# A two-layer transformer trunk: four mixed weight pairs per chunk instead of three, one weight sum made by an adding DMA, and a new layout of the weights

## The chip, the cores and the metric

The kernel runs on one core of one Trainium2 chip. The metric is the time of one execution on the device in microseconds (us). The engines are named as in the profile: PE multiplies matrices, DVE and ACT work element by element, POOL is GpSimd, and SP issues most of the DMAs.

## The reference

Two layers, each with a mixer (two kinds of attention between an input and an output projection) and a SwiGLU block, all in float32 on 256 tokens of width 2048. The change touches the SwiGLU block and the way in which weights are loaded:

```python
D_MODEL = 2048; SEQ = 256; DEPTH = 2
D_FF = (-(-8 * D_MODEL // 3) + 255) // 256 * 256          # 5632

def swiglu(h, w_gate, w_up, w_down):
    return (jax.nn.silu(h @ w_gate) * (h @ w_up)) @ w_down

for l in range(DEPTH):
    h = rms_norm(x, pre_mix_norm[l])
    m = hybrid_mixer(h, l, w_in[l], w_o[l], ...)
    x = x + rms_norm(m, post_mix_norm[l])
    h = rms_norm(x, pre_ffn_norm[l])
    f = swiglu(h, w_gate[l], w_up[l], w_down[l])
    x = x + rms_norm(f, post_ffn_norm[l])
```

## The kernel before

**Splitting.** A float32 operand goes to PE in two parts: ACT rounds it to the multiplier's format (`hi`, L176), DVE subtracts (`lo = raw - hi`, L178), and a product of an activation (sh, sl) with a weight (hi, lo) is three matmuls: sh·hi, sh·lo, sl·hi (`product`, L706 to L708; `unit` in the projections, L352 to L354).

**Weights.** All weights stand in one list, `stream`, in the order of use. An entry is a pair of K tiles: 256 rows by 512 columns, 512 KB, which SP loads into a tile `raw` of 128 partitions by 2 x 512 (L139). There are four `raw` tiles; a load waits until one is free again, that is, until `lo` or the last sum that reads it is done. There are six `hi` and six `lo` tiles. `feed` splits up to four entries ahead of the one that is used (`LOOKAHEAD`). The tile framework plans the order in which each engine issues its instructions; each engine then runs its own list strictly in that order and waits by semaphores.

**Gate and up.** The 5632 columns are done in 11 chunks of 512. In a chunk, for each of 8 K pairs `kp`, a gate entry and an up entry are used. The plain way (`eight`) is eight products (2 K tiles x 2 token tiles x gate and up), 24 matmuls. The other way (`seven`) takes the 2 x 2 blocks of tokens and K tiles against K tiles and gate/up as a 2 x 2 matrix product by Strassen's scheme in Winograd's form: seven products, 21 matmuls. For that it needs four sums of activations, made once per pair and layer (`pair_sums`, `token_sums`), and four sums of weights per chunk and pair (`mixed_weights`). With g0, g1 the two K tiles of gate and u0, u1 those of up they are t1 = g0 + u0, t3 = u0 + u1, t2 = t1 + u1, t4 = t2 + g1. DVE adds them (L150) into tiles `T`, and ACT and DVE split them into `Th` (L159) and `Tl` (L161); u1 is split alone (L154, L155). In chunk 0 the pairs 4 and 6 go by seven products (`FIRST_SEVEN`), in the chunks 1 to 10 the pairs 2, 4 and 6 (`SEVEN`). Four of the seven products are shared by several outputs; they add up in banks of their own (p1, p6, p7, q5) over the pairs of a chunk, and `shared_part` and the end of the chunk add them to the four results (L743 to L747, L853 to L856). Four banks serve the results of a chunk and the other four its shared products, and the roles change with each chunk.

**Down.** Two halves of 1024 columns; in each, 6 of the 22 pairs (`DOWN_SEVEN`) go by seven products, with the weights mixed by the same function.

**Order around the change.** SP issues the loads in stream order. ACT issues `hi`, then for a mixed entry `Th`; DVE issues the sums, `lo` and `Tl`. POOL makes masks at the opening and applies the rotation of the differential heads (`rotate`, L570 to L573), and issues no DMA.

The program's function and its callers:

Of the kernel before, what the change touches and what calls it, by code (L numbers as in the profile page):

```python
# [9 lines left out]
F32 = mybir.dt.float32  # L10
# [7 lines left out]
P = 128  # L18
D = 2048
S = 256  # L20
L = 2
# [14 lines left out]
SEVEN = (2, 4, 6)  # L36
FIRST_SEVEN = (4, 6)
FIRST_ORDER = (0, 1, 3, 2, 4, 5, 6, 7)
FORM_AT = {1: 4, 3: 6, 5: 2}
# [9 lines left out]

@with_exitstack  # L50
def kernel(
# [3 lines left out]
    w_in: bass.AP,  # L55
    w_o: bass.AP,
# [6 lines left out]
    w_gate: bass.AP,  # L63
    w_up: bass.AP,
    w_down: bass.AP,
    rope: bass.AP,
    x_columns: bass.AP,
    gain_columns: bass.AP,
    out: bass.AP,
# [21 lines left out]
    stream = []  # L91

    def queue_pair(w2d, kp, c):
        stream.append(
            w2d[kp * 2 * P : (kp + 1) * 2 * P, c * CW : (c + 1) * CW].rearrange("(k p) n -> p k n", p=P)
        )
        return len(stream) - 1

    plan = []
    sevens = set()  # L100
    for l in range(L):
        lay = {"in": {}, "o": {}, "gate": {}, "up": {}, "down": {}}
        chunks = []
        for g in range(2):
            chunks += [6 + g, 8 + g, 10 + g]
        for g in range(2):
            chunks += [g, 2 + g, 4 + g]
        lay["chunks"] = chunks
        for c in chunks:
            for kp in range(KT // 2):  # L110
                lay["in"][c, kp] = queue_pair(w_in[l], kp, c)
        order_o = [(c, kp) for kp in KP_O for c in (0, 1)]
        order_o += [(c, kp) for c in (2, 3) for kp in range(KT // 2)]
        lay["order_o"] = order_o
        for c, kp in order_o:
            lay["o"][c, kp] = queue_pair(w_o[l], kp, c)
        for c in range(FF // CW):
            for kp in FIRST_ORDER if c == 0 else range(KT // 2):
                lay["gate"][c, kp] = queue_pair(w_gate[l], kp, c)
                lay["up"][c, kp] = queue_pair(w_up[l], kp, c)  # L120
                if kp in (FIRST_SEVEN if c == 0 else SEVEN):
                    sevens.add(lay["up"][c, kp])
        for half in range(2):
            for kp in range(FF // P // 2):
                for c in (2 * half, 2 * half + 1):
                    lay["down"][c, kp] = queue_pair(w_down[l], kp, c)
                if kp in DOWN_SEVEN:
                    sevens.add(lay["down"][2 * half + 1, kp])
        plan.append(lay)
# [5 lines left out]
    def fetch(upto):  # L135
        while len(raws) < min(upto, len(stream)):
            i = len(raws)
            raw = wpool.tile([P, 2, CW], F32, tag="raw", bufs=4, name=f"raw{i}")
            loads.append(nc.sync.dma_start(raw, stream[i]))  # L139
            raws.append(raw)  # L140
# [3 lines left out]
    def mixed_weights(i):  # L144

        g, u = raws[i - 1], raws[i]
        sums = [mix_pool[0].tile([P, 2, CW], F32, tag="T", bufs=2, name=f"T{i}_{j}") for j in range(2)]
        t1, t3, t2, t4 = sums[0][:, 0, :], sums[0][:, 1, :], sums[1][:, 0, :], sums[1][:, 1, :]
        for o, a, b in ((t1, g[:, 0, :], u[:, 0, :]), (t3, u[:, 0, :], u[:, 1, :]), (t2, t1, u[:, 1, :]), (t4, t2, g[:, 1, :])):
            nc.vector.tensor_tensor(out=o, in0=a, in1=b, op=ALU.add)  # L150
        parts = []
        hi = wpool.tile([P, 2, CW], F32R, tag="hi", bufs=6, name=f"hi{i}")
        lo = wpool.tile([P, 2, CW], F32R, tag="lo", bufs=6, name=f"lo{i}")
        nc.scalar.activation(hi[:, 1, :], u[:, 1, :], AF.Copy)  # L154
        nc.vector.tensor_tensor(out=lo[:, 1, :], in0=u[:, 1, :], in1=hi[:, 1, :].bitcast(F32), op=ALU.subtract)  # L155
        parts.append((hi[:, 1, :], lo[:, 1, :]))
        for j in range(2):
            th = mix_pool[0].tile([P, 2, CW], F32R, tag="Th", bufs=3, name=f"Th{i}_{j}")
            nc.scalar.activation(th, sums[j], AF.Copy)  # L159
            tl = mix_pool[0].tile([P, 2, CW], F32R, tag="Tl", bufs=3, name=f"Tl{i}_{j}")  # L160
            nc.vector.tensor_tensor(out=tl, in0=sums[j], in1=th.bitcast(F32), op=ALU.subtract)  # L161
# [53 lines left out]
    setup = tc.alloc_tile_pool(name="setup", bufs=1, side="right", reuse_waits="tile")  # L215
    idle = setup.tile([P, CW], BF16, name="idle")
# [10 lines left out]
    lams = setup.tile([P, 4, L * 64], F32, name="lams")  # L227
    negones = setup.tile([P, P], F32, name="negones")
# [6 lines left out]
    def late_constants():  # L235
# [16 lines left out]
        lprod = setup.tile([P, 2, L * 64], F32, name="lprod")  # L252
        lsum = setup.tile([P, 2, L], F32, name="lsum")
# [761 lines left out]
```

## Time and profile before

| | us |
|---|---|
| median of three runs (lowest, highest) | 2225.18 (2224.80, 2225.68) |
| the profiled execution, its time on the device | 2225.4 |
| its span, first to last instruction | 2223.6 |
| first gate and up stage, from its first matmul to the first of down | 402.3 to 877.1 |
| second gate and up stage, first to last matmul | 1509.8 to 1982.4 |

The mean granted PE clock over the span is 0.998. A row of the profile names line, engine, operation, output and inputs, and shape; "mean ns of one" runs from an instruction's start to its end, and instructions of an engine can overlap, so their distance can be shorter than that. "Idle before" is the time that the engine stood before these instructions, with what ended it. A row of windows gives the busy time of each engine between two times.

### The profile page before, as it was taken

Reading aid. Unit: us, or ns where it says so; the run is one execution under the profiler, and the core shown is the slowest. Engines: PE = TensorE matmul, PEld = TensorE weight load, DVE = VectorE, ACT = ScalarE, POOL = GpSimd, SP = SyncE. Lnnn points to the kernel's source line nnn. Section 1 sums busy time; section 2 is a strip of 40 time slices with the busy share of each in tenths; the row PEclk is TensorE's granted clock in tenths of the full one; section 3 lists DMA queues with packets and bytes.
Section 4 is the critical chain, followed back from the end, with each engine's and each line's share of the span. In section 5 each row is a group of like instructions: output and inputs, shape, how many; then the busy total and the mean of one; then the engine's idle time right before and its main releaser. Section 6 shows DMA issues by size and latency. Waiting matters only on the chain.

```text
span 2223.6 us, 28156 instructions
## 1 busy us (share of the span) xinstructions
PE 2205.6 (99%) x10117; PEld 1814.4 (82%) x10117; DVE 1765.9 (79%) x2505; ACT 1276.3 (57%) x1895; POOL 37.4 (2%) x76
## 2 busy tenths in 40 slices
PE   9999999999999999999999999999999999999998
PEld 7888888788888888888877888887888888888886
DVE  6666555899889989989876665558998898999897
ACT  6555554656555556656565455546655555566563
POOL 1100000000000000000010000000000000000000
PEclk9999999999999999999999999999999999999999
DMA  8655555466665665656555555554666565566564
GB/s 292 194 164 165 159 189 183 138 208 203 204 199 190 205 207 189 213 189 213 194 182 170 169 163 161 183 187 151 201 207 202 178 221 194 190 212 211 183 217 143
DMA packets 217996, 423.72 MB, mean 191 GB/s; under 512 B 13568, under 2 KB 14080, under 8 KB 217344
## 3 DMA queue, kind: packets, MB, share of 16 engines
q1 hardware_dynamic: 217712, 421.91, 58.8%
q8 instruction: 79, 1.29, 0.2%
q14 instruction: 61, 0.50, 0.1%
q10 hardware_dynamic: 144, 0.02, 0.0%
HBM read 419.77 MB, written 2.10 MB: 190 GB/s over the span
## 4 chain that ended last, share of the span: by engine, by line
PE 94%; ACT 2%; DVE 1%; DMA 1%; issue 0%; SPq 0%; DVEq 0%; ACTq 0%
PE c L707 10%; PE c L706 10%; PE c L708 10%; PE in L352 8%; PE in L354 8%; PE in L353 8%; PE dn L911 5%; PE dn L909 5%; PE dn L908 5%; PE o L354 2%; PE o L352 2%; PE o L353 2%; PE p L706 2%; PE p L707 2%; PE p L708 2%; ACT hi L176 1%
## 5 line engine op out<-in xcount | busy, mean ns | idle before, releaser
L178 DVE TENSOR_TENSOR lo<-raw,hi 128x1024 fp32r<-128x1024 f32 x695 | 843.9, 1224 | 309.6 <-ACT hi L176 304.4
L176 ACT ACTIVATE hi<-raw 128x1024 fp32r<-128x1024 f32 x695 | 726.9, 1056 | 497.8 <-PE in L354 164.9
L706 PE MATMUL c<-hi,xF 128*128 128x512 f32 x960 | 377.0, 394 | 1.4 <-ACT w L743 0.8
L707 PE MATMUL c<-lo,xF 128*128 128x512 f32 x960 | 373.9, 390 | 1.1 <-DVE lo L178 1.0
L708 PE MATMUL c<-hi,xF 128*128 128x512 f32 x960 | 374.0, 391 | 0.0
L159 ACT ACTIVATE Th<-T 128x1024 fp32r<-128x1024 f32 x176 | 185.7, 1056 | 141.7 <-DVE T L150 133.8
L161 DVE TENSOR_TENSOR Tl<-T,Th 128x1024 fp32r<-128x1024 f32 x176 | 214.2, 1217 | 4.4 <-ACT Th L159 3.8
L706 PEld LDWEIGHTS c<-hi,xF 128*128 128x128 f32 x960 | 180.5, 188 | 39.2 <-ACT w L743 1.2
L707 PEld LDWEIGHTS c<-lo,xF 128*128 128x128 f32 x960 | 180.6, 188 | 38.5 <-DVE lo L178 2.3
L708 PEld LDWEIGHTS c<-hi,xF 128*128 128x128 f32 x960 | 180.7, 188 | 37.8
L908 PE MATMUL dn<-hi,jh 128*128 128x512 f32 x464 | 180.7, 389 | 0.0
L909 PE MATMUL dn<-lo,jh 128*128 128x512 f32 x464 | 180.5, 389 | 0.0
L352 PE MATMUL in<-hi,xI 128*128 128x512 f32 x384 | 154.0, 401 | 0.4 <-ACT xI L293 0.4
L352 PE MATMUL in<-hi,xT 128*128 128x512 f32 x384 | 153.8, 401 | 0.5 <-ACT hi L176 0.5
L354 PE MATMUL in<-hi,xI 128*128 128x512 f32 x384 | 150.3, 391 | 0.3 <-DVE xI L298 0.3
L353 PE MATMUL in<-lo,xI 128*128 128x512 f32 x384 | 150.0, 391 | 0.5 <-DVE lo L178 0.5
L353 PE MATMUL in<-lo,xT 128*128 128x512 f32 x384 | 149.8, 390 | 0.5 <-DVE lo L178 0.5
L354 PE MATMUL in<-hi,xT 128*128 128x512 f32 x384 | 150.1, 391 | 0.0
L911 PE MATMUL dn<-hi,jl 128*128 128x512 f32 x464 | 142.8, 389 | 0.0
L150 DVE TENSOR_TENSOR T<-T,raw 128x512 f32<-128x512 f32 x176 | 120.5, 684 | 1.2
L911 PEld LDWEIGHTS dn<-hi,jl 128*128 128x128 f32 x464 | 87.1, 188 | 18.1
L908 PEld LDWEIGHTS dn<-hi,jh 128*128 128x128 f32 x464 | 87.1, 188 | 18.1
(295 smaller groups left out, 3513.8 us busy)
## 6 DMA issues: line engine op xcount, KB each, us to landing
raw<-in_w_in_dram SPq DMA_DIRECT2D x191, 512.0 KB, 3.8
raw<-in_w_gate_dram SPq DMA_DIRECT2D x176, 512.0 KB, 3.8
raw<-in_w_up_dram SPq DMA_DIRECT2D x176, 512.0 KB, 4.5
raw<-in_w_down_dram SPq DMA_DIRECT2D x176, 512.0 KB, 4.5
raw<-in_w_o_dram SPq DMA_DIRECT2D x64, 512.0 KB, 4.0
xr<-in_x_columns_dram SPq DMA_DIRECT2D x8, 256.0 KB, 6.9
x<-in_x_dram SPq DMA_DIRECT2D x4, 512.0 KB, 8.6
gpost_mix<-in_post_mix_norm_dram SPq DMA_DIRECT2D x2, 1024.0 KB, 6.9
```

The costliest lines, as they stand in the source:

```text
L161: nc.vector.tensor_tensor(out=tl, in0=sums[j], in1=th.bitcast(F32), op=ALU.subtract)
L176: nc.scalar.activation(hi, raw, AF.Copy)
L178: nc.vector.tensor_tensor(out=lo, in0=raw, in1=hi.bitcast(F32), op=ALU.subtract)
L352: nc.tensor.matmul(a, sh, hi[:, kk, :], start=first and kk == 0, stop=False)
L353: nc.tensor.matmul(a, sh, lo[:, kk, :], start=False, stop=False)
L354: nc.tensor.matmul(a, sl, hi[:, kk, :], start=False, stop=last and kk == 1)
L706: nc.tensor.matmul(a, sh, hi, start=first, stop=False)
L707: nc.tensor.matmul(a, sh, lo, start=False, stop=False)
L708: nc.tensor.matmul(a, sl, hi, start=False, stop=last)
L908: nc.tensor.matmul(accs[c, t], sh, hi[:, kk, :], start=first, stop=False)
L909: nc.tensor.matmul(accs[c, t], sh, lo[:, kk, :], start=False, stop=False)
L911: nc.tensor.matmul(accs[c, t], sl, hi[:, kk, :], start=False, stop=last)
```

## The change

- `SEVEN` becomes (1, 3, 4, 6): four pairs by seven products in the chunks 1 to 10. Chunk 0 and down keep theirs. Chunk 0 now makes the token sums of pairs 3 and 1 as well (`FORM_AT`), four pairs instead of three.
- The sum t1 = g0 + u0 is made by a DMA that POOL issues: behind the load of an up entry that is to be mixed, it adds the first half of the gate entry from DRAM onto the first half of the up tile. This holds for down's mixed entries too.
- The other sums are written in place: t2 = t1 + u1 over u1 (after u1 is split), t3 = t2 - g0 over g0, t4 = t2 + g1 over g1. The tiles `T` go. The up tile is split as a whole (t1 and u1), then t2, then t3 and t4 together; `Th` and `Tl` are two tiles of three halves instead of three of two.
- There are six `raw` tiles instead of four.
- The host lays all weights out in one array `weights_in_turn`, in stream order, each entry as 128 partitions x 4 KB without a gap. The four weight arrays go as inputs.
- Storage: the pool `setup` goes (its constants take tiles `t2` of the attention pool, the tile `idle` a `lo` tile), `rotate` has one buffer per tile instead of two, and the token sums of down lie in the pool of the sums.

```diff
-SEVEN = (2, 4, 6)
+SEVEN = (1, 3, 4, 6)
 FIRST_SEVEN = (4, 6)
 FIRST_ORDER = (0, 1, 3, 2, 4, 5, 6, 7)
-FORM_AT = {1: 4, 3: 6, 5: 2}
+FORM_AT = {1: 4, 3: 6, 4: 3, 5: 1}
...
+def weights_laid_out(inputs):
+    order = weight_order()[0]
+    out = np.empty((len(order), P, 2 * CW), np.float32)
+    for o, (name, l, kp, c) in zip(out, order):
+        w = inputs[name][l, kp * 2 * P : (kp + 1) * 2 * P, c * CW : (c + 1) * CW]
+        o[...] = w.reshape(2, P, CW).transpose(1, 0, 2).reshape(P, 2 * CW)
+    return out
...
+    order, plan, sevens = weight_order()
+    stream = [weights_in_turn[i].rearrange("p (k n) -> p k n", k=2) for i in range(len(order))]
...
     def fetch(upto):
         while len(raws) < min(upto, len(stream)):
             i = len(raws)
-            raw = wpool.tile([P, 2, CW], F32, tag="raw", bufs=4, name=f"raw{i}")
+            raw = wpool.tile([P, 2, CW], F32, tag="raw", bufs=6, name=f"raw{i}")
             loads.append(nc.sync.dma_start(raw, stream[i]))
+            if i in sevens:
+                nc.gpsimd.dma_start(raw[:, 0, :], stream[i - 1][:, 0, :], accum_op=ALU.add)
             raws.append(raw)
...
     def mixed_weights(i):
         g, u = raws[i - 1], raws[i]
-        sums = [mix_pool[0].tile([P, 2, CW], F32, tag="T", bufs=2, name=f"T{i}_{j}") for j in range(2)]
-        t1, t3, t2, t4 = sums[0][:, 0, :], sums[0][:, 1, :], sums[1][:, 0, :], sums[1][:, 1, :]
-        for o, a, b in ((t1, g[:, 0, :], u[:, 0, :]), (t3, u[:, 0, :], u[:, 1, :]), (t2, t1, u[:, 1, :]), (t4, t2, g[:, 1, :])):
-            nc.vector.tensor_tensor(out=o, in0=a, in1=b, op=ALU.add)
-        parts = []
         hi = wpool.tile([P, 2, CW], F32R, tag="hi", bufs=6, name=f"hi{i}")
         lo = wpool.tile([P, 2, CW], F32R, tag="lo", bufs=6, name=f"lo{i}")
-        nc.scalar.activation(hi[:, 1, :], u[:, 1, :], AF.Copy)
-        nc.vector.tensor_tensor(out=lo[:, 1, :], in0=u[:, 1, :], in1=hi[:, 1, :].bitcast(F32), op=ALU.subtract)
-        parts.append((hi[:, 1, :], lo[:, 1, :]))
-        for j in range(2):
-            th = mix_pool[0].tile([P, 2, CW], F32R, tag="Th", bufs=3, name=f"Th{i}_{j}")
-            nc.scalar.activation(th, sums[j], AF.Copy)
-            tl = mix_pool[0].tile([P, 2, CW], F32R, tag="Tl", bufs=3, name=f"Tl{i}_{j}")
-            nc.vector.tensor_tensor(out=tl, in0=sums[j], in1=th.bitcast(F32), op=ALU.subtract)
-            parts += [(th[:, k, :], tl[:, k, :]) for k in range(2)]
-        b22, t1, t3, t2, t4 = parts
+        th = mix_pool[0].tile([P, 3, CW], F32R, tag="Th", bufs=2, name=f"Th{i}")
+        tl = mix_pool[0].tile([P, 3, CW], F32R, tag="Tl", bufs=2, name=f"Tl{i}")
+
+        def split(h, l, w):
+            nc.scalar.activation(h, w, AF.Copy)
+            nc.vector.tensor_tensor(out=l, in0=w, in1=h.bitcast(F32), op=ALU.subtract)
+
+        split(hi, lo, u)
+        t2 = u[:, 1, :]
+        nc.vector.tensor_tensor(out=t2, in0=u[:, 0, :], in1=t2, op=ALU.add)
+        nc.vector.tensor_tensor(out=g[:, 0, :], in0=t2, in1=g[:, 0, :], op=ALU.subtract)
+        nc.vector.tensor_tensor(out=g[:, 1, :], in0=t2, in1=g[:, 1, :], op=ALU.add)
+        split(th[:, 2, :], tl[:, 2, :], t2)
+        split(th[:, 0:2, :], tl[:, 0:2, :], g)
+        t1, b22 = ((hi[:, k, :], lo[:, k, :]) for k in range(2))
+        t3, t4, t2 = ((th[:, k, :], tl[:, k, :]) for k in range(3))
         return {"b22": b22, "t1": t1, "t2": t2, "t3": t3, "t4": t4}
...
-    idle = setup.tile([P, CW], BF16, name="idle")
+    idle = wpool.tile([P, CW], BF16, tag="lo", bufs=6, name="idle")
...
-        ra = pool.tile([P, NH, 16], F32, tag="ra", bufs=2, name=f"ra_{nm}")
-        rb = pool.tile([P, NH, 16], F32, tag="rb", bufs=2, name=f"rb_{nm}")
+        ra = pool.tile([P, NH, 16], F32, tag="ra", bufs=1, name=f"ra_{nm}")
+        rb = pool.tile([P, NH, 16], F32, tag="rb", bufs=1, name=f"rb_{nm}")
...
-                    forms[kp] = token_sums(pool, dn, 2, a11, a12, a21, a22, f"{l}_{half}_{kp}")
+                    forms[kp] = token_sums(pool, mix_pool[0], 2, a11, a12, a21, a22, f"{l}_{half}_{kp}")
```

More of the change, by code (lines that the diff above doesn't have):

```diff
@@ L88, in four_banks @@
         return [make(n) for make, n in zip(makers, names)]
[L91 to L129, printed above, removed]
+    order, plan, sevens = weight_order()
+    stream = [weights_in_turn[i].rearrange("p (k n) -> p k n", k=2) for i in range(len(order))]
     ready = {}
@@ L251, in late_constants @@
         nc.gpsimd.memset(lamsign, 1.0)
[L252 to L253 removed]
+        lprod = pool.tile([P, 2, L * 64], F32, tag="t2", name="lprod")
+        lsum = pool.tile([P, 2, L], F32, tag="t2", name="lsum")
         for i in range(2):
@@ L591, in split @@
             )
-        raw = wpool.tile([P, 2, CW], F32, tag="raw", bufs=4, name="raw0")
+        raw = wpool.tile([P, 2, CW], F32, tag="raw", bufs=6, name="raw0")
         hi = wpool.tile([P, 2, CW], F32R, tag="hi", bufs=6, name="hi0")
@@ L622, in settle @@
             yield 1
-        late_constants()
-        setup.release()
+        late_constants(pool)
         rs += [inv_rms(t, pool, "in0") for t in range(NT)]
@@ L1003 @@
     feeds += list(zip(("x_columns", "gain_columns"), _columns(inputs)))
+    feeds += [("weights_in_turn", weights_laid_out({k: _np.asarray(v) for k, v in inputs.items()}))]
     for name, a in feeds:
```

55 lines of the change are left out of this document (44 added, 11 removed).

## The prediction

> **What bounds the kernel now.** I read the page first (busy times and the chain), then the windows by stage, then the timeline of one chunk of gate and up, then who waits for whom.
>
> ```profile
> span 2223.6 us, 28156 instructions
> PE 2205.6 (99%) x10117; PEld 1814.4 (82%) x10117; DVE 1765.9 (79%) x2505; ACT 1276.3 (57%) x1895; POOL 37.4 (2%) x76
> PE 94%; ACT 2%; DVE 1%; DMA 1%; issue 0%; SPq 0%; DVEq 0%; ACTq 0%
> L178 DVE TENSOR_TENSOR lo<-raw,hi 128x1024 fp32r<-128x1024 f32 x695 | 843.9, 1224 | 309.6 <-ACT hi L176 304.4
> L176 ACT ACTIVATE hi<-raw 128x1024 fp32r<-128x1024 f32 x695 | 726.9, 1056 | 497.8 <-PE in L354 164.9
> L706 PE MATMUL c<-hi,xF 128*128 128x512 f32 x960 | 377.0, 394 | 1.4 <-ACT w L743 0.8
> L161 DVE TENSOR_TENSOR Tl<-T,Th 128x1024 fp32r<-128x1024 f32 x176 | 214.2, 1217 | 4.4 <-ACT Th L159 3.8
> ```
>
> PE is busy 99% of the span and is 94% of the chain. Taking matmuls away therefore pays as long as the operands still come in time. The 394 ns of a matmul are not its price, since matmuls overlap; the price is the distance between two starts. These two rows of the timeline of PE are 14 matmuls apart, with only 128x512 matmuls between:
>
> ```profile
> 600.16 0.39 PE L706 MATMUL c<-hi,xF 128*128 128x512 f32 x1
> ...
> 603.33 0.39 PE L708 MATMUL c<-hi,xF 128*128 128x512 f32 x1
> ```
>
> 3.17 / 14 = 0.226 us. Whoever takes 0.39 comes to a saving 1.7 times too large.
>
> ```profile
> core 0: us, PE busy (x) PEld busy (x) DVE busy (x) ACT busy (x) POOL busy (x), PEclk, DMA share, GB/s
> 411.00:456.00 45.00, 42.62 (x177) 33.24 (x178) 39.57 (x81) 28.47 (x51) 0.00 (x0) 0.96 0.56 170
> 456.00:856.00 400.00, 400.00 (x1804) 331.04 (x1803) 360.90 (x430) 224.03 (x258) 0.00 (x0) 1.00 0.62 200
> 1517.00:1562.00 45.00, 42.79 (x190) 33.51 (x190) 41.62 (x85) 30.20 (x55) 0.00 (x0) 1.00 0.57 179
> 613.06:655.48 42.42, 42.42 (x192) 35.13 (x191) 37.43 (x45) 23.38 (x28) 0.00 (x0) 1.00 0.61 200
> ```
>
> The windows show the two starts of gate and up (411 to 456, 1517 to 1562), the steady part of the first, and one chunk of 42.42 us. In the steady part PE has no hole at the full granted clock, and DVE is the next engine with 37.43 of 42.42 us. Only at the starts does PE lose something: 2.4 and 2.2 us.
>
> ```profile
> ACT hi L176 <- PE c L708: 8.7, 5, 4.4
> DVE lo L178 <- ACT hi L176: 7.6, 2, 4.1
> DVE T L150 <- DMA raw<-in_w_up_dram: 0.5, 1, 0.5
> ```
>
> These are the waits inside that chunk. ACT's longest wait is for PE to give back a hi tile, and DVE then waits for ACT: the preparation is ahead as far as its six hi tiles let it be. DVE's 5.0 idle us are back-pressure, not a shortage.
>
> **The change, part by part.**
>
> *Matmuls.* A pair by eight products is 24 matmuls, by seven 21. Chunks 1 to 10 of both layers get one more pair by seven: 20 x 3 = 60 matmuls, 60 x 0.226 = 13.6 us off PE. Chunk 0 and down keep their number.
>
> *DVE.* Its price is again the distance of starts:
>
> ```profile
> 617.91 1.21 DVE L178 TENSOR_TENSOR lo<-raw,hi 128x1024 fp32r<-128x1024 f32 x1
> 619.04 0.68 DVE L746 TENSOR_TENSOR w<-q,w 128x512 f32<-128x512 f32 x1
> 619.64 0.68 DVE L747 TENSOR_TENSOR w<-q,w 128x512 f32<-128x512 f32 x1
> ```
>
> 1.13 us for 1024 columns, 0.60 for 512. A mixed up tile costs now 4 sums, one lo of 512 and two Tl of 1024: 5 x 0.60 + 2 x 1.13 = 5.26. After: three sums, one Tl of 512, a lo and a Tl of 1024: 4 x 0.60 + 2 x 1.13 = 4.66. A chunk had 3 x 5.26 and five plain lo of 1.13 (21.4), and gets 4 x 4.66 and four plain lo (23.2): 1.8 more. 37.4 + 1.8 = 39.2 in a chunk of 42.42 - 3 x 0.226 = 41.74. That leaves DVE 2.5 idle us instead of 5.0. It fits, so its cost on the path is zero; the cover is the lead of the preparation. ACT rounds 2560 columns for a mixed tile before and after; with one more mixed tile it stays far below PE. In down DVE gets lighter.
>
> *The transfer that adds.* For each of the 108 mixed tiles POOL now adds 256 KB of gate weights onto the landed up tile. The wait is new: POOL waits for the up load; ACT's hi and DVE's lo of that tile wait for POOL's transfer, and behind them stand, in order, all later splits. In the gate and up stages nothing else is queued on POOL.
>
> ```profile
> raw<-in_w_up_dram SPq DMA_DIRECT2D x176, 512.0 KB, 4.5
> out_dram<-x SPq DMA_DIRECT2D x8, 256.0 KB, 2.3
> DMA to landing us min/median/max: 3.5/4.3/9.6
> SPq L139 <- DVE lo L178: 1289.3, 570, 6.3
> ```
>
> No transfer of this kind is in the trace. Call A the time from the landing of the up tile to the landing of the sum. The nearest rows put it between 2.3 (a 256 KB store) and 9.6 (the slowest weight load). It takes in 256 KB and touches 256 KB that lie there already, 512 KB in all, so I take the up load's 4.5. The Trainium skill (Collectives: The Full Stack, The bandwidth ceiling: the fold count and why AG ≠ RS ≠ AR) says that an adding transfer is slowed by its two source reads, not by the add; no run here shows it yet. Its page DMA: Bandwidth & Descriptors (Anatomy of one DMA — SWDGE (gpsimd) path) gives 2.0 us plus bytes / 436e3, so an estimate of 2.6 us for 256 KB, with which the sum would be the same 13.6; the trace's loads take longer than that fit (3.2 for 512 KB against 4.5).
>
> Does A fit? The last row above shows what a load waits for: SP waits 1289 us in all until DVE's lo gives a raw tile back. So raw tile, load, sum, splits and release form a loop. I follow the tightest part in PE's time, from the start of a chunk, with pairs of 24 x 0.226 = 5.4 and 21 x 0.226 = 4.75 us. Pair 6 starts at 30.6, and its first product with an in-place sum is the fourth of seven, at 32.6. Pair 1's last Tl stands on DVE behind the additions of the chunk before, and ends about 1.3. By the order of the changed program pair 4's up load takes that raw tile: issue 1.5, landing 6.0, sum at 6.0 + A. Then hi 1.06, lo 1.22, and pair 3's last Tl 1.22, which the order puts behind that lo: 9.5 + A. Pair 6's up load takes that tile: landing at 9.7 + 4.5 + A = 14.2 + A, sum at 14.2 + 2A. Its own chain is hi 1.06, lo 1.22, three sums 1.8, Th 1.06, Tl 1.22, and on DVE some 1.7 more for the two plain lo of pair 7 that stand between: 8.1. So 22.3 + 2A must not pass 32.6: A may be 5.15. With 4.5 there is 1.3 us to spare and PE does not wait. Beyond 5.15 each us of A costs 2 us in each of 20 chunks, 40 us in all. In down a mixed tile comes every third pair and the same reckoning leaves more room.
>
> *Six raw tiles instead of four, weights laid out in order of use.* Loads wait for raw tiles and land in time; in the steady stages nothing waits on them but the 0.5 us per chunk above, so this pays nothing there. Layout and tiles act at the opening and at the starts.
>
> *The starts of gate and up.*
>
> ```profile
> PE c L707 <- DVE Tl L161: 1.6, 2, 0.8
> PE c L706 <- ACT w L743: 0.8, 1, 0.8
> ACT hi L176 <- DMA raw<-in_w_gate_dram: 25.6, 20, 2.5
> ```
>
> PE waits there for the first Tl and for w, and behind these ACT waits for loads that found no free raw tile. Two more tiles help. Against that DVE forms the token sums of four pairs instead of three (two sums of 128x256, four of 128x128, one of 128x512: about 2.1 us) and has 1.8 us more in chunk 1. Bounds: all 4.6 us of the two starts vanish, or 2 x 3.9 = 7.8 are added. I take zero, as the two have like size.
>
> *The rest* (constants in tiles of t2, one pair of rotation buffers, token sums of down in another pool) moves storage; POOL does the rotation in order anyway. Zero, hidden behind a PE with no hole in attention.
>
> **Sum.** The profiled execution took 2225.4 us, 1.8 beside its span and 0.2 above the median of the runs. 2225.4 - 13.6 = 2211.8; against the median 2211.6. Forecast 2212.
>
> **The rivals.**
>
> 1. *The sum comes too late* (slower). If A passes 5.15, pair 6 waits in each chunk, and at A = 5.5 the 14 us of cost have eaten the gain. At 6.2 it is 42 - 14, so 2253. For it: the stretch is bursty (DMA share 0.62, in bursts near full), and the row's maximum is 9.6. Against: the median is 4.5, and the new layout gives a load one run of 4 KB per partition instead of two of 2 KB. Chance 0.20.
>
> 2. *POOL is held up by DVE* (slower). Two rows of the same POOL operation:
>
> ```profile
> 56.43 0.46 POOL L573 TENSOR_TENSOR tok<-ra,rb 128x128 f32<-128x128 f32 x1
> 57.95 1.32 POOL L573 TENSOR_TENSOR tok<-ra,rb 128x128 f32<-128x128 f32 x1
> ```
>
> It takes 0.46 or 1.32, and the 0.86 more is less than one DVE operation of 1024 columns (1.22). If the making of a transfer meets two such holds, A is 4.5 + 1.7 = 6.2 and the time is again 2253. The Trainium skill (SBUF — State Buffer, SBUF: two separate sides) calls it a trap that a DVE operation in a two-port mode keeps GpSimd from writing descriptors. Its page VectorE: DVE Perf Modes (Why `tensor_tensor` can't do 2×_2P or 4×) excludes that mode for operations with two input tensors. The trace agrees with this so far: the splits and sums have two inputs and take 1.13 us for 1024 columns and 0.60 for 512, which is one pace, about one column in 1.04 ns, and nothing faster. Chance 0.03.
>
> 3. *DVE becomes the bound* (slower). It needs 39.2 of 41.7. If the 5.0 idle us stay, because ACT and DVE wait in order for each other, a chunk takes 44.2 instead of 42.42: 20 x 1.8 = 36, so 2261; it decides where more than 3.2 us stay. The waits say that the idle time is back-pressure. Chance 0.04.
>
> 4. *The starts eat part.* With the upper bound there, 13.6 - 7.8 = 5.8: 2219. DVE is already busy for 39.6 and 41.6 of 45 us there. Chance 0.10.
>
> 5. *The starts get better.* With the lower bound, 13.6 + 4.6: 2207. Chance 0.07.
>
> **How the numbers follow.** The forecast (2207 to 2217) has the remaining 0.56. Differences of 0.2%, 4.4 us, are about what a measurement of this kernel can tell from none. Faster by more (below 2220.7): 0.56 + 0.07 + half of case 4 = 0.68. Within: the other half of case 4 and 0.03 of case 1 = 0.08. Slower: 0.24. The range goes from 2206 to 2240: it leaves out the upper part of cases 1 to 3 (A above 5.9) and the tip of case 5. For the forecast alone it is 2207 to 2217.
>
> **What would show it.** Right: 60 fewer 128x512 matmuls, a chunk of about 41.7 us, DVE near 39 in it, PE without a hole, the sum's transfer at 3 to 5 us. Wrong: holes of PE in front of Th or Tl in pair 6 with ACT's hi waiting for the adding transfer (case 1), POOL's issue long after the landing (case 2), DVE full while PE waits (case 3), or a matmul distance other than 0.226.

## The result: 14% slower, and the profile after

The changed kernel takes 2546.8 us (median) against 2225.4 for the kernel before: 1.144 times as long, 95% interval 1.142 to 1.146. The forecast was 2212 with a range up to 2240. So the result lies far outside the range, on the side of rival 1 (the sum comes too late), and at many times its price.

The page of the changed kernel, profiled in an execution of 2547.3 us; lines of the old kernel have moved (the load is now L152, the transfer that adds L154, the splits of a mixed tile L168 and L169, the sums in place L173 to L175, the plain splits L192 and L194, PE's product L720 to L722):

```profile
span 2545.6 us, 28575 instructions
PE 2322.8 (91%) x10057; PEld 1853.7 (73%) x10057; DVE 1783.8 (70%) x2531; ACT 1295.9 (51%) x1937; POOL 133.9 (5%) x184
raw<-in_weights_in_turn_dram SPq DMA_DIRECT2D x783, 512.0 KB, 4.0
raw<-in_weights_in_turn_dram POOLq DMA_DIRECT2D x108, 256.0 KB, 6.8
```

The 60 matmuls are gone (10117 to 10057), yet PE falls from 99% to 91%, and DVE and ACT fall too: nobody is the bound, everybody waits. The last two rows give the median time from issue to landing: 4.0 us for a load of 512 KB, 6.8 us for an adding transfer of 256 KB.

The windows of the changed kernel, one chunk of gate and up, the steady stretch, and one of down (columns as in the prediction):

```profile
core 0: us, PE busy (x) PEld busy (x) DVE busy (x) ACT busy (x) POOL busy (x), PEclk, DMA share, GB/s
616.47:669.30 52.83, 47.49 (x192) 37.69 (x191) 39.86 (x48) 25.26 (x30) 3.46 (x5) 0.92 0.58 178
560.00:800.00 240.00, 208.31 (x834) 162.44 (x833) 174.36 (x208) 110.13 (x130) 16.53 (x19) 0.92 0.57 174
900.00:1080.00 180.00, 162.59 (x680) 129.38 (x679) 139.22 (x183) 92.62 (x115) 9.59 (x11) 0.95 0.59 192
```

A chunk is 52.8 us long instead of 42.4, with 39.9 us of DVE in it, about the 39.2 that the prediction gave it. PE's granted clock falls to 0.92.

By stage (from its first to its last matmul, us):

| | gate, up, layer 0 | layer 1 | down, layer 0 | layer 1 |
|---|---|---|---|---|
| before | 474.9 | 472.8 | 232.7 | 232.3 |
| after | 598.8 | 595.2 | 269.5 | 271.5 |

Gate and up pay 246 us and down 76; together that is the whole 322 by which the span grew. Attention is unchanged.

The waits of the changed kernel (who waited for whom: us in total, times, longest):

```profile
ACT hi L168 <- DMA raw<-in_weights_in_turn_dram: 521.5, 76, 10.2
DVE lo L169 <- ACT hi L168: 357.1, 66, 7.7
PE p L720 <- ACT Th L168: 50.2, 22, 4.4
PE p L721 <- DVE Tl L169: 33.8, 38, 1.7
```

ACT waits 521 us for the adding transfers, DVE waits for ACT behind that, and PE for the tiles of sums. That is rival 1's sign. Why it costs so much is seen when one chunk is followed in the timeline (start, duration, engine; in brackets the idle time before and what ended it):

```profile
623.60 1.06 ACT L168 ACTIVATE hi<-raw 128x1024 fp32r<-128x1024 f32 x1 [6.60 <-DMA raw<-in_weights_in_turn_dram]
...
631.24 1.21 DVE L169 TENSOR_TENSOR Tl<-raw,Th 128x1024 fp32r<-128x1024 f32 x1
...
632.48 0.33 SPq L152 DMA_DIRECT2D raw<-in_weights_in_turn_dram  x1
...
636.31 0.86 POOL L154 DMA_DIRECT2D raw<-in_weights_in_turn_dram  x1 [10.19 <-DMA raw<-in_weights_in_turn_dram]
...
643.06 1.06 ACT L168 ACTIVATE hi<-raw 128x1024 fp32r<-128x1024 f32 x1 [4.77 <-DMA raw<-in_weights_in_turn_dram]
...
646.42 1.22 DVE L169 TENSOR_TENSOR Tl<-raw,Th 128x1024 fp32r<-128x1024 f32 x1
...
647.67 0.33 SPq L152 DMA_DIRECT2D raw<-in_weights_in_turn_dram  x1
...
651.68 0.86 POOL L154 DMA_DIRECT2D raw<-in_weights_in_turn_dram  x1 [14.51 <-DVE Tl L169]
...
658.72 1.06 ACT L168 ACTIVATE hi<-raw 128x1024 fp32r<-128x1024 f32 x1 [6.91 <-DMA raw<-in_weights_in_turn_dram]
...
664.02 1.22 DVE L194 TENSOR_TENSOR lo<-raw,hi 128x1024 fp32r<-128x1024 f32 x1
...
665.27 0.33 SPq L152 DMA_DIRECT2D raw<-in_weights_in_turn_dram  x1
...
669.30 0.89 POOL L154 DMA_DIRECT2D raw<-in_weights_in_turn_dram  x1 [16.75 <-DVE lo L194]
...
676.33 1.06 ACT L168 ACTIVATE hi<-raw 128x1024 fp32r<-128x1024 f32 x1 [7.80 <-PE c L722]
```

Read it as a relay. Pair 1's sum lets ACT's hi start at 623.60; its last Tl ends at 632.45 and sets a raw tile free. The load of pair 4's up tile starts at 632.48 into that tile, the transfer at 636.31, and ACT's hi at 643.06. Pair 3's last Tl, behind that on DVE, ends at 647.64, and the load for pair 6 starts at 647.67; its hi starts at 658.72. A plain lo behind it ends at 665.24, and the load for pair 1 of the next chunk starts at 665.27; its hi starts at 676.33. Now the chain is where it began, 52.7 us later. The brackets name the last event that the profile saw before a start, and some of them mislead. Where POOL's rows name DVE, the up load had landed 0.7 us before (650.97 and 668.57). And the last row names PE, but pair 1's sum had landed at 676.16, the usual 0.16 us before its hi; by the order of the six hi tiles the tile that this hi takes had last been read by PE in pair 6, up to 670.41. So PE is nowhere in the chain. It is a closed loop of three legs, each a load and A (from the landing of the up tile to the landing of the sum), with ACT's and DVE's steps between them: 32.2 us in the legs and 20.5 in the steps, a sum's landing taken 0.16 us ahead of its hi.

It is the same in all 18 chunks 2 to 10 of the two layers (the first is 0): the up load of pair 4 starts 0.03 us after pair 1's last Tl ends, that of pair 6 after pair 3's last Tl, that of the next pair 1 after the lo of pair 7's up tile, which stands on DVE behind pair 6's sums, and ACT's hi of these three pairs starts 0.16 us after its sum has landed. Pair 3's sum, which is in no leg, lies ready for 5.8 us on the mean.

### The profile page after: what moved, and what is told of

Read it like the earlier page. It is cut to its first block, busy times and chain, and to the rows that moved or that the text cites. A ratio compares the mean times of both kernels' runs of the same rounds, so it can differ in the third digit from the quotient of the medians.

```text
span 2545.6 us, 28575 instructions
## 1 busy us (share of the span) xinstructions
PE 2322.8 (91%) x10057; PEld 1853.7 (73%) x10057; DVE 1783.8 (70%) x2531; ACT 1295.9 (51%) x1937; POOL 133.9 (5%) x184
## 5 line engine op out<-in xcount | busy, mean ns | idle before, releaser
L194 DVE TENSOR_TENSOR lo<-raw,hi 128x1024 fp32r<-128x1024 f32 x675 | 814.5, 1221 | 223.0 <-ACT hi L192 219.1
L192 ACT ACTIVATE hi<-raw 128x1024 fp32r<-128x1024 f32 x675 | 698.4, 1052 | 314.9 <-PE in L369 169.1
L168 ACT ACTIVATE hi<-raw 128x1024 fp32r<-128x1024 f32 x108 | 114.2, 1057 | 573.0 <-DMA raw<-in_weights_in_turn_dram 521.5
L169 DVE TENSOR_TENSOR lo<-raw,hi 128x1024 fp32r<-128x1024 f32 x108 | 131.9, 1221 | 357.1 <-ACT hi L168 357.1
L720 PE MATMUL c<-hi,xF 128*128 128x512 f32 x820 | 328.1, 402 | 31.6 <-DVE w L761 21.4
L721 PE MATMUL c<-lo,xF 128*128 128x512 f32 x820 | 324.8, 396 | 0.0
L722 PE MATMUL c<-hi,xF 128*128 128x512 f32 x820 | 323.1, 396 | 0.0
L168 ACT ACTIVATE Th<-raw 128x512 fp32r<-128x512 f32 x216 | 179.6, 839 | 175.6 <-DVE raw L173 140.8
L169 DVE TENSOR_TENSOR Tl<-raw,Th 128x512 fp32r<-128x512 f32 x216 | 204.3, 951 | 49.0 <-ACT Th L168 49.0
L720 PEld LDWEIGHTS c<-hi,xF 128*128 128x128 f32 x820 | 158.6, 193 | 74.0 <-DVE w L761 28.6
L154 POOL DMA_DIRECT2D raw<-in_weights_in_turn_dram x108 | 94.1, 871 | 2096.5 <-DMA raw<-in_weights_in_turn_dram 824.0
L722 PEld LDWEIGHTS c<-hi,xF 128*128 128x128 f32 x820 | 157.4, 192 | 33.8
L721 PEld LDWEIGHTS c<-lo,xF 128*128 128x128 f32 x820 | 157.8, 192 | 33.0
```

What stands on the lines that cost most here:

```text
L168: nc.scalar.activation(h, w, AF.Copy)
L169: nc.vector.tensor_tensor(out=l, in0=w, in1=h.bitcast(F32), op=ALU.subtract)
L192: nc.scalar.activation(hi, raw, AF.Copy)
L194: nc.vector.tensor_tensor(out=lo, in0=raw, in1=hi.bitcast(F32), op=ALU.subtract)
L720: nc.tensor.matmul(a, sh, hi, start=first, stop=False)
L721: nc.tensor.matmul(a, sh, lo, start=False, stop=False)
```

## The experiments

"The changed kernel" is the one of the diff above. Ratios are against the kernel before, on the same chip, with a 95% interval.

**Is it the transfer?** The sum made by DVE instead:

```
-                nc.gpsimd.dma_start(raw[:, 0, :], stream[i - 1][:, 0, :], accum_op=ALU.add)
...
+        nc.vector.tensor_tensor(out=u[:, 0, :], in0=u[:, 0, :], in1=g[:, 0, :], op=ALU.add)
```

> The changed kernel with one edit: the sum t1 = u0 + g0 is made in place by DVE instead of by the transfer that adds (108 sums of 0.60 us; no transfer on POOL's queue). All else stays: four pairs by seven, in-place sums, six raw tiles, the new layout. Theory (the transfers' latency, 7.5 us from the landing of the up tile to the landing of the sum where I had taken 4.5, is what costs 321 us): the cost goes, the 60 matmuls stay away; DVE has 39.2 + 4 x 0.60 = 41.6 us in a chunk of 41.74, on its limit, so 2212 to 2240. Rival A (the sums in place hold raw tiles too long): still above 2400. Rival B (the fourth pair by seven itself, through DVE's load and the token sums): still above 2400.

2256.3 us (ratio 1.0138, 1.0124 to 1.0151). The transfers cost 290 of the 321 us; rivals A and B fall. The 31 that stay above 2225 I put down to DVE, which has the sums now. Its window over more than five chunks:

```profile
560.00:800.00 240.00, 237.56 (x1051) 191.48 (x1050) 229.04 (x279) 138.54 (x160) 0.00 (x0) 1.00 0.59 199
```

DVE is busy 95% of it, and behind the first two a chunk takes 43.0 us on the mean, not 41.74. So this time missed the expected 2240: an engine that would be 41.6 of 41.7 us busy does not reach that.

The same with three pairs by seven:

```
-SEVEN = (1, 3, 4, 6)
+SEVEN = (2, 4, 6)
-FORM_AT = {1: 4, 3: 6, 4: 3, 5: 1}
+FORM_AT = {1: 4, 3: 6, 5: 2}
```

> As the kernel with DVE's in-place sum, but with the old choice of pairs (2, 4, 6 by seven, as before the change): layout in order of use, six raw tiles, in-place sums and the merged tile of three sums, without transfers. Matmuls as before the change. Theory: 2219 to 2229, level with the kernel before (2225), as nothing of it touched PE. Rival A (in-place sums hold raw tiles): above 2350, since three of eight pairs still do it. Rival B (the fourth pair): 2225 as well.

2220.5 us (ratio 0.9979, 0.9970 to 0.9988), as expected; a little faster than before. The gain is at the starts of gate and up: the first two chunks (from the stage's first matmul to the first of the third chunk) took 88.4 us together in layer 0 and 88.2 in layer 1, against 93.0 and 90.9 before, 7.3 us in all. The later chunks took back 0.9 of it and down 1.7. Six raw tiles, sums in place and the layout are no loss.

Three pairs by seven, with transfers (the same choice of pairs in the changed kernel):

> The changed kernel with the old choice of pairs (2, 4, 6 by seven), transfers kept. Theory: each transfer in a chunk costs its share of the 11 us that a chunk is longer than 42, so three cost about 8.5 in a chunk: 2225 + 22 x 8.5 + 76 (down, as in the changed kernel) = about 2490, between 2440 and 2530. Rival A (sums in place): the same, 2490. Rival B (the fourth pair overloads DVE): 2225 to 2300, for it is gone.

2316.9 us (ratio 1.041, 1.0391 to 1.0429): far below what the theory expected, and above Rival B's range. Its windows, gate and up first, then down:

```profile
560.00:800.00 240.00, 240.00 (x1080) 198.74 (x1079) 204.15 (x233) 133.57 (x151) 14.80 (x17) 1.00 0.70 223
900.00:1080.00 180.00, 165.09 (x684) 131.86 (x683) 134.86 (x189) 91.26 (x119) 7.85 (x9) 0.96 0.60 188
```

In the steady chunks of gate and up PE has no hole at all, with three transfers in each. So a transfer does not cost its share; pairs 2, 4, 6 leave PE in charge and 1, 3, 4, 6 do not. The trace shows why: here only two legs are left. In all 20 chunks 1 to 10 the up load of pair 6 waits for pair 2's last Tl, and from chunk 2 on that of pair 2 for the last Tl of pair 6 in the chunk before, but pair 4's load waits for a plain lo, of pair 1. The loop of two just fits: ACT still waits 0.8 us for pair 2's sum on the mean, and pair 6's lies ready for 0.9. Down, which is the same as in the changed kernel, has all of its holes: 269.9 and 269.4 us. Rival B is not saved by this, since the fourth pair without transfers took 2256.

**The size of a leg.** The transfer in two halves:

```
+                for h in (slice(0, CW // 2), slice(CW // 2, CW)):
+                    nc.gpsimd.dma_start(raw[:, 0, h], stream[i - 1][:, 0, h], accum_op=ALU.add)
```

> The changed kernel with the adding transfer cut in two of 256 columns each, issued one after the other: POOL's second issue adds at least 0.87 us to A. A dose. Theory (three legs in a chunk, one leg in each of 24 transfers of down): 21 x 3 x 0.87 + 24 x 0.87 = 76, so 2620, and more if A grows more: in each chunk the period grows by three times what A grows. By the prediction's two legs per chunk 2603; if only the last transfer of a chunk counted 2585; if latency is not what counts 2540 to 2555.

2598.9 us (1.168, 1.1655 to 1.1698). By the time alone this is nearest to the 2603 of two legs, so it decides nothing; A grew by 0.2 to 0.7 us, less than the 0.87 that I had expected (table below). And the transfer as a plain copy, which leaves the adding out:

```
-nc.gpsimd.dma_start(raw[:, 0, :], stream[i - 1][:, 0, :], accum_op=ALU.add)
+nc.gpsimd.dma_start(raw[:, 0, :], stream[i - 1][:, 0, :])
```

> The changed kernel with the transfer as a plain copy: the adding is left out, so the operand t1 is g0 alone. All else stays. It tells what of A is the adding. The adding packets take 178 ns for 2048 B, the plain ones of before took 84, eight packets on each of 16 engines: 0.75 us less per transfer, so 21 x 3 x 0.75 + 24 x 0.75 = 65 and 2481 if only the packets' own time counts. If the two source reads make up all of A beyond a plain transfer (A 2.5 to 3.5), the loop falls below PE's pace: 2205 to 2260. If it is the queue and the issue through POOL, whatever they carry: 2530 to 2550.

2436.2 us (1.0945, 1.0925 to 1.0965); between the cases, as a leg got 1.35 us shorter. For the three legs of a chunk, means over the steady chunks of both layers, from issues and landings in the trace (us):

| | three loads | three A (pairs 1, 4, 6) | period of a chunk | rest |
|---|---|---|---|---|
| plain copy | 10.6 | 6.9 + 5.6 + 6.5 | 50.0 | 20.4 |
| changed kernel | 10.6 | 8.1 + 7.0 + 8.0 | 54.0 | 20.4 |
| two halves | 10.9 | 8.5 + 7.2 + 8.7 | 55.4 | 20.1 |

The rest is the same within 0.3 us, and it is the 20.5 of ACT's and DVE's steps that the timeline showed. Counted chunk by chunk, from one landing of pair 1's sum to the next, it is 20.47 to 20.51 us in each of 16 chunks of the changed kernel and 20.48 to 20.51 with the copy. So the period is three loads plus three A plus 20.4, and each us of A costs 3 us in a chunk. In down a mixed tile comes every third pair and there is one leg for each: load 4.4, A 7.6, rest 7.8, period 19.8 in the changed kernel; 4.5, 6.2, 8.0 and 18.7 with the copy (means; in the changed kernel the rest is 7.2 to 7.5 in 18 of the 20 intervals and 12.4 or 12.5 in the first of each second half). PE needs 69 matmuls of 0.226 us, 15.6, for three pairs.

**Where the loop closes.** Five raw tiles:

```
-            raw = wpool.tile([P, 2, CW], F32, tag="raw", bufs=6, name=f"raw{i}")
+            raw = wpool.tile([P, 2, CW], F32, tag="raw", bufs=5, name=f"raw{i}")
```

> The changed kernel with five raw tiles instead of six. Theory (the raw tiles are the store that the transfers' latency uses up: 16 tiles of a chunk, each held for 6 x 53 / 16 = 20 us on the mean): with five a chunk comes to between 53 and 53 x 6 / 5 = 64 us, I expect 60, so 2546 + 22 x 7 + some 40 in down = 2740, at least 2640. If the store is not what limits (DVE's or ACT's own work does, or POOL's issues): 2546 to 2580.

2582.5 us, in one run: the expectation failed. The time a tile is held isn't fixed: A of the four pairs came to 25.1 us instead of 27.4, I suppose because fewer loads were in flight. One tile less did little while the loop stayed closed. The other direction:

```
-tag="raw", bufs=6   -tag="hi", bufs=6   -tag="lo", bufs=6
+tag="raw", bufs=8   +tag="hi", bufs=5   +tag="lo", bufs=5
```

> The changed kernel with eight raw tiles, and five hi and five lo tiles instead of six, which keeps the storage the same. Theory (a closed loop, because the load of a mixed tile takes a raw tile that the sums of the mixed tile before set free): two more tiles lead a load back to a release that does not hang on the latest sum, so the loop opens, in down as well, and PE or DVE sets the pace: a chunk of 42 to 45 us instead of 54, so 2230 to 2320. Rival (what limits is ACT and DVE waiting in order behind a late sum, however many raw tiles there are): above 2450.

2243.5 us (1.0076, 1.0058 to 1.0095). Two more raw tiles, at the cost of a hi and a lo tile, take away 303 us. A is still 7.3 us in pair 1 and 6.9 in pair 6 on the mean, but nothing waits for it: in the chunks 2 to 10 every sum lies ready for 0.9 to 13 us before its hi, pair 4's load waits for a plain lo, of pair 0, and PE is busy all of the steady stretch.

```profile
560.00:800.00 240.00, 240.00 (x1069) 195.59 (x1069) 224.82 (x265) 144.37 (x165) 20.02 (x23) 1.00 0.75 224
```

The up tile of a mixed pair loaded before the gate tile, with six raw tiles as in the changed kernel:

```
+            for j in (i + 1, i) if i + 1 in sevens else (i,):
+                raw = pair[j] = wpool.tile([P, 2, CW], F32, tag="raw", bufs=6, name=f"raw{j}")
+                loads.append(nc.sync.dma_start(raw, stream[j]))
```

> The changed kernel with one edit: of a mixed pair the up tile is loaded before the gate tile, so it takes the raw tile that comes free first, and its transfer can begin sooner. Theory (loop of three legs): the two loads of a mixed pair started 2.3, 2.3 and 3.1 us apart in the chunk that I followed, so the loop is 7.7 us shorter, 53 to 46: 2546 - 22 x 7.7 = 2377, and with some 2 us for each of 24 transfers in down 2330; between 2290 and 2400. Rival (the transfers fill DMA engines or hold ACT up by their number, wherever they start): 2520 to 2560.

2294.1 us (1.0307, 1.0288 to 1.0326): a chunk takes 43.7 us. Only the order of two loads was changed. The loop is shorter, not open: the up loads of pairs 4 and 6 now wait for the short Tl of 512 columns of pairs 1 and 3, which ends 2.3 us before the last one does, A has fallen to 4.5 in pair 4, and the rest to 16.3 us. ACT's hi of pairs 1 and 6 still starts 0.16 to 0.18 us after the landing in all 18 chunks, and in down nearly all of them do so too (down takes 245.5 and 245.7 us). And both at once:

> Both at once: eight raw tiles with five hi and lo tiles, and the up tile of a mixed pair loaded before the gate tile; four pairs by seven with the adding transfer. Theory: the sums then lie ready, ACT does not wait for them, and the time is the forecast's 2212 up to 2235 (DVE's 39.2 us of 41.7 and its waits). If five hi and lo tiles or DVE's order limit: 2235 to 2290. If latency is not what limits: above 2300.

2243.7 us (1.0078, 1.0062 to 1.0093), level with eight raw tiles alone: with eight the loop is open in either order, and the expected 2235 failed for another reason.

**What transfers do by themselves.** Transfers that nobody waits for:

```
+                nc.gpsimd.tensor_copy(scrap[:, 0:1], raw[:, 0, 0:1])
+                nc.gpsimd.dma_start(scrap, stream[i - 1][:, 0, :], accum_op=ALU.add)
```

> The kernel with three pairs by seven and DVE's in-place sums (2220.5 us), and beside it, at the same places and of the same size, 88 adding transfers into a tile of their own that nobody reads; POOL copies one column of the up tile first, so that each starts when the up tile has landed. Five hi tiles instead of six make room for that tile. It separates what the transfers do to the loads and engines from the waiting for their result. Theory (only the waiting for the sum counts): 2218 to 2230. Rival (the transfers slow the loads, DVE or POOL by themselves): most of the 96 us between the kernels with three transfers (2317) and with none (2220.5), so above 2270.

2238.7 us (1.0054, 1.0041 to 1.0068): above the theory's 2230 and far below 2270. In the steady chunks the transfers cost nothing: 42.4 us each, as without them. Two controls without any transfer show what the rest was. Eight raw and five hi and lo tiles:

> The kernel with three pairs by seven and DVE's in-place sums (2220.5 us), with eight raw tiles and five hi and five lo tiles; no transfer. It is the control for the 23 us by which the changed kernel with eight raw tiles (2243.5) is above 2220.5 in spite of 60 fewer matmuls. If five hi and lo tiles cost them (each entry into layer 1 had a hole of 6.5 us, and single matmuls in down started 338 ns apart): 2235 to 2245. If the transfers themselves do (they share the DMA engines with the loads): 2219 to 2227.

2245.7 us (1.0098, 1.0083 to 1.0113). Seven raw, six hi and five lo tiles:

> Control for the kernel with the up tile first, seven raw tiles, six hi and five lo tiles (2230.5 us): three pairs by seven, DVE's in-place sums, no transfer, with the same seven raw, six hi and five lo tiles. If five lo tiles cost by themselves (up to the 25 us of five hi and lo): 2225 to 2235, and the fourth pair with its transfer is worth little or nothing. If they cost nothing: 2219 to 2223, level with the kernel of six each (2220.5), and the fourth pair costs some 10 us even with its sums in time.

2244.0 us (1.0083, 1.0069 to 1.0096), above both expectations. So a lo tile less, or a hi and a lo tile less, costs 23 to 25 us with no transfer at all, beside one or two raw tiles more, which weren't tried by themselves. That is enough to cover the 18 us of the idle transfers and all that eight raw tiles left over 2220; a hi tile less by itself was not tried.

**The sum on POOL, in SBUF:**

```
-nc.gpsimd.dma_start(raw[:, 0, :], stream[i - 1][:, 0, :], accum_op=ALU.add)
+nc.gpsimd.tensor_tensor(out=raw[:, 0, :], in0=raw[:, 0, :], in1=raws[i - 1][:, 0, :], op=ALU.add)
```

> The changed kernel with one edit: POOL adds g0 to u0 in SBUF (one tensor_tensor of 128x512 in place per mixed tile) instead of issuing the transfer. DVE keeps its 39.2 us of a chunk. Theory (a closed loop of three legs per chunk, each a load of 3.2 to 3.8 us plus A, the time from the up tile's landing to its sum, and 20.4 us of ACT's and DVE's steps between them: 54 us with A 7.7): with A of 1 to 2.5 us the loop is 33 to 39 us, below PE's 41.7, so PE sets the pace again: 2205 to 2216. Rival (POOL and DVE share something, so DVE's 39.2 us grow beyond 41.7): 2225 to 2280.

2281.8 us (1.0252, 1.0238 to 1.0266): the rival's side, 2 us above its range. Groups by line, of this kernel first, then of the kernel with DVE's sum and three pairs, whose L173 is the same operation (busy, mean ns of one):

```profile
L154 POOL TENSOR_TENSOR raw<-raw,raw 128x512 f32<-128x512 f32 x108 | 331.9, 3073 | 1605.9 <-DMA raw<-in_weights_in_turn_dram 1124.9 <-DVE rsq_o_p L295 274.1 <-DVE lo L194 152.9
L174 DVE TENSOR_TENSOR raw<-raw,raw 128x512 f32<-128x512 f32 x108 | 95.3, 883 | 2.1
```

```profile
L173 DVE TENSOR_TENSOR raw<-raw,raw 128x512 f32<-128x512 f32 x88 | 60.5, 687 | 1.3
```

These means mix two kinds. The durations in ns (min/median/max) of the same two lines:

```profile
L154 POOL TENSOR_TENSOR raw<-raw,raw x108: 1282/2294/6574, 407.9 to 2234.1; 128x512 f32<-128x512 f32 x108
L174 DVE TENSOR_TENSOR raw<-raw,raw x108: 675/692/1662, 426.0 to 2241.2; 128x512 f32<-128x512 f32 x108
```

Of DVE's 108 sums 82 take 675 to 695 ns, as they do without POOL's sum, and 26 take 1.19 to 1.66 us. POOL's sum takes 1.28 us at least and 6.57 at most: one from 643.30 on runs for 6.1 us beside six DVE operations in a row, the last of which takes 1.66 us instead of 0.69. So here POOL and DVE do hold each other up. For transfers this is not so: POOL issued the 108 of the changed kernel in 853 to 1011 ns each.

**Versions.** Four pairs in every second chunk, DVE's sums, no transfer:

```
+MORE = (1, 2, 4, 6)
...
+            mine = FIRST_SEVEN if c == 0 else SEVEN if c % 2 else MORE
```

> The kernel with DVE's in-place sums and no transfer, with pairs 1, 2, 4, 6 by seven in every second chunk (2, 4, ... 10) and 2, 4, 6 in the others: 30 matmuls fewer than before. DVE needs 41.6 us of 41.74 in the former, 37.4 of 42.42 in the latter. If the lead of the preparation carries the heavy chunk over: 2220.5 - 30 x 0.226 = 2213.7. If each heavy chunk takes the 43.7 us that the kernel with four pairs and DVE's sums took: 2220.5 + 10 x 1.3 = 2233. I expect 2216 to 2224.

2230.2 us (1.0018, 1.0009 to 1.0027): from first matmul to first matmul, the chunks with four pairs took 42.6 to 44.3 us instead of 41.7, and those with three behind the start 42.4 to 42.7. So the lead of the preparation does not carry them over.

The up tile first with seven raw, six hi and five lo tiles:

> The changed kernel with the up tile of a mixed pair loaded first, seven raw tiles, six hi and five lo tiles. Theory: in gate and up the loop of three legs has about 40 us with six raw tiles and less with seven, so it is open, and in down a leg reaches back one tile more; with six hi tiles ACT keeps its lead: 2212 to 2238. If five lo tiles limit as five hi and lo did: 2240 to 2246. If seven raw tiles leave the loop closed in down: 2250 to 2290.

2230.5 us (1.0025, 1.0015 to 1.0034). With down's sums by DVE:

> The same (up tile first, seven raw tiles, six hi, five lo), but in down DVE makes the sums and only the 84 mixed tiles of gate and up have the transfer. If down's transfers are what is left of the cost: down back at 233 us per layer, so at or below the run with transfers in down by up to 24 us, and 2212 to 2230 in all. If down's loop was open already: the same as that run within 5 us.

2231.2 us (1.0029, 1.0018 to 1.0040), the same: down's loop was open already.

The up tile first, seven raw tiles and six of hi and of lo; the space comes from scratch:

```
-name=f"att{l}", bufs=6      -name=f"ffn{l}", bufs=6
+name=f"att{l}", bufs=4      +name=f"ffn{l}", bufs=5
```

> The changed kernel with the up tile of a mixed pair loaded first, seven raw tiles and six hi and six lo tiles; the storage comes from the tiles of scratch (t2): four instead of six in attention, five instead of six in the FFN stages. Five lo tiles had cost 23.5 us by themselves (2244.0 against 2220.5), and with them the kernel with the up tile first had 2230.5, so 13.5 less than its control. If both add up: 2220.5 - 13.5 = 2207, and 2204 to 2215 in all, below the kernel before. If fewer scratch tiles cost in attention or at the starts of gate and up: 2215 to 2245.

2219.3 us (0.9973, 0.9962 to 0.9984): faster than before by 6 us, with all four pairs and all 108 transfers.

```profile
560.00:800.00 240.00, 240.00 (x1080) 197.57 (x1079) 223.66 (x263) 143.06 (x166) 20.07 (x23) 1.00 0.73 227
900.00:1080.00 180.00, 180.00 (x795) 148.79 (x794) 158.73 (x217) 111.75 (x144) 7.86 (x9) 1.00 0.67 219
```

PE is full in both stages. In gate and up the sums lie ready for 3.0 to 8.3 us on the mean, pair by pair, and in down for 4.8 at least. The expected 2207 failed, since the two controls' difference did not add up: against the kernel with DVE's sums and three pairs (2220.5) a steady chunk is 0.55 us shorter, 42.43 to 41.88, and the 18 chunks behind the starts 9.0 us in all, but the first two chunks together are 4.8 us longer in layer 0 and 4.0 in layer 1. So gate and up come out level, and the 1.3 us between the two medians, which their intervals do not part, stand in down (233.0 and 232.5 us against 233.6 and 233.2). Of the longer starts only 0.5 to 0.6 us is in the first chunk of each layer (46.1 against 45.5 and 45.6), as it is in the run with four pairs in turn (46.1 and 46.2), which has six scratch tiles and makes the same number of token sums. The rest is in the second, the first with four mixed pairs (47.0 and 46.1 against 42.9 and 42.6). What the scratch tiles add was not tried.

## Why the prediction was wrong, step by step

- **Matmuls: nearly right.** 60 went. With the loop open a chunk gains 0.53 us on the kernel before (42.41 to 41.88), not 0.68. Most matmuls start 227 ns apart there as before, but in the products by seven single steps are longer, in layer 0 up to 0.34 us; why was not followed.
- **DVE at 39.2 us: right.** 223.66 of 240 in the last run is 39.0 us of a chunk of 41.88, and PE is full. Rival 3 did not come, but DVE has no more room: at 41 us a chunk takes 43.
- **A: too small.** I took 4.5, and gave 9.6 as the upper end. The three legs have 8.1, 7.0 and 8.0. Alone on the DMA engines the transfer takes 3.6 us from issue to landing, which with 0.7 us before the issue is A = 4.4; but loads are in flight beside it. That my 4.5, the median of a 512 KB load among other loads, is so near the 4.4 is luck. The estimate of 2.6 us for 256 KB that the prediction drew from the Trainium skill (DMA: Bandwidth & Descriptors, Anatomy of one DMA — SWDGE (gpsimd) path) is near what the plain copy took alone, 2.9; with loads in flight the trace does not agree.
- **The loop: the step that failed.** The forecast's term "PE does not wait" for the transfers stood on it. I followed two legs, from a chunk's start to pair 6, and let pair 1 be in time at 1.3 us by PE's clock. But pair 1's raw tile is set free behind the sums of pair 6 of the chunk before: a third leg, which closes the loop. So there was nothing by which A "may be 5.15". By the measured law, 41.7 - 20.4 - 10.6 leaves 10.7 for three A: 3.6 each. The shortest A in the trace is 4.2. At my own 4.5 a chunk would have taken 44.5 us: with A at 4.5 in every leg the forecast was wrong all the same. And the price is 3 us per us and chunk, not 2.
- **"In down the same reckoning leaves more room": wrong.** One leg per mixed tile must fit in 15.6 us, and 15.6 - 4.4 - 7.8 leaves 3.4. Down cost 76 us more.
- **Size of rival 1.** Its sign came as written, at a chance of 0.20, but not its size. It stood at A = 6.2 and 2253; by its price of 40 us for each us beyond 5.15, an A of 7.7 would have given 2314. With A 7.7, three legs and down: 20 chunks of 54.0 instead of 41.7 are 246; in down the four halves have five intervals between mixed tiles each, 20 x (19.8 - 15.6) = 84; and 2225 - 14 + 246 + 84 = 2541. Measured: 2547. It is so near in part by luck: by stage the sum is 14 too low in gate and up (232 against 246) and 8 too high in down (84 against 76).
- **Rival 2: did not come for transfers.** All 108 issues came 0.5 to 1.1 us after the up load's landing and took 853 to 1011 ns, so the Trainium skill's trap (SBUF — State Buffer, SBUF: two separate sides) was rightly given little. The same section says that a DVE operation with two SBUF inputs contends with a GpSimd operation that reads SBUF, and the run with POOL's sum agrees: 26 of DVE's 108 sums took 1.19 us and more instead of 0.69.
- **Raw tiles, layout and starts: zero was the sum of two real sizes.** The tiles, layout and sums in place gave 7.3 us at the starts (the run with three pairs and DVE's sums), rival 5's side. The fourth pair and what goes with it took 8.7 there (the last run against that one), rival 4's mechanism. In the changed kernel the loop's cost covers both.
- **PE's clock** at 0.92 in these chunks is a result: PE stands in no leg of the loop, whose parts add up to the period without it. That is argued; no run changed the clock alone.

That pairs 2, 4 and 6 leave PE in charge with A of 7.7, 4.3 and 6.0 fits this: their loop has two legs in a chunk, not three. Another order of ACT's and DVE's lists, which would change the 20.4 us of steps, was not tried.

## What to carry to other kernels

When tiles are reused in order of release, follow the reuse around until it meets itself before pricing a latency: if a load needs a tile that the last late result sets free, the period is the sum of the loop, no engine's busy time shows it, and each us counts once per leg. A loop is shortened by order and opened by tiles: swapping two loads gave back 253 of 321 us, two more raw tiles 303, and once nothing in the loop waits the same latency costs nothing. Look also at what an added tile is paid with: one lo tile less cost 23 us in the kernel with DVE's sums, and 11 with the transfers (2230.5 against 2219.3, where scratch tiles paid for it).

## What the runs showed of the hardware

Time from issue to landing of the 256 KB transfer, by the number of weight loads in flight at any moment between 0.5 and 2.5 us after its issue (means, from the trace; the five and six transfers beside one or three loads are left out):

| loads in flight | adding (changed kernel) | plain copy |
|---|---|---|
| 0 | 3.64 us (21 transfers) | 2.88 (20) |
| 2 | 6.12 (23) | 4.74 (22) |
| 4 | 7.32 (59) | 5.88 (60) |

```profile
L154 POOL DMA_DIRECT2D raw<-in_weights_in_turn_dram x108: 853/866/1011, 407.7 to 2494.2; - x108
DMA to landing us min/median/max: 3.6/6.8/9.8
```

```profile
L154 POOL DMA_DIRECT2D raw<-in_weights_in_turn_dram x108: 536/536/709, 411.6 to 2386.0; - x108
DMA to landing us min/median/max: 2.8/5.4/6.9
```

The first pair of rows is the adding transfer, the second the plain copy (ns min/median/max of POOL's issue, then landing). Adding costs 0.8 us alone and 1.4 beside four loads, 0.33 of it in the issue. The Trainium skill (Collectives: The Full Stack, The bandwidth ceiling: the fold count and why AG ≠ RS ≠ AR) says of the adding transfers of a reduce-scatter that two source reads slow them down, not the add. No run here parts the two; but half of the 7.3 us (7.32 - 3.64) comes with the other loads, which a plain copy meets as well (5.88 - 2.88).
